# One block of level products per scan segment, from copies of each level's keys and queries

## The chip, the cores and the metric

The kernel runs on one core of a Trainium2 chip. The metric is the device time of one execution in microseconds (us). It is float32 in and out. One core has five engines that matter here, each with its own queue of instructions: PE multiplies matrices (PEld are its weight loads), DVE and ACT work on whole tiles of 128 partitions, POOL does a few copies, and SP issues the transfers (DMA).

## The reference: what is computed

One layer works on 2048 tokens of 1024 channels, with 256 context tokens ahead of them. After a modulated norm, one large projection gives the inputs of a gated linear recurrence (HGRN2, eight heads of 128 channels, both directions) and of a gated short convolution; a second projection brings both back, and a residual and a norm end it. The part that the change touches is the recurrence:

```python
bcum = jnp.cumsum(gc, axis=2)
diff = bcum[:, :, :, None, :] - bcum[:, :, None, :, :]
decay = jnp.where(mask, jnp.exp(jnp.where(mask, diff, 0.0)), 0.0)
attn = jnp.einsum('bhtk,bhsk,bhtsk->bhts', qc, kc, decay)
o = jnp.einsum('bhts,bhsv->bhtv', attn, vc) + jnp.einsum('bhtk,bhkv->bhtv', qc * jnp.exp(bcum), S)
```

For two tokens t and s of a chunk, attn is the product of query and key with a decay that depends on the channel and on all gates between s and t. The same is done backwards, and both directions are added.

## The kernel before, in words

**Stages.** The first 115 us load, norm and transpose the input. Then 32 windows follow, one for each head and each group of 512 tokens (a segment). In each window PE computes the projections of one segment, gates and values (and for some windows the output gates), while the scan of the segment before it is worked in between. After the heads come the convolution's windows (to about 1900 us) and the output projection.

**Projections.** Each f32 product is made of three f16 products (high x high, high x low, low x high), and each block of four is made of seven products by a Strassen-like scheme (`seven`, L830, its matmuls L839 to L841). One product is 4 x 3 = 12 matmuls of 128 x 256. Three PSUM banks of their own (sa, sb, sc) take them. ACT copies intermediate results out (`keep`, L844, its activation L846: tiles p and u) and DVE makes the outputs (L850). A product that adds to a bank can start only when the copy of what the bank held is made, and there is one other product between the two.

**The scan of a segment.** The products with decay are made in levels. At level lev, blocks of B = 2^lev tokens are paired. Keys and queries hold two copies, one for each direction (K and Q, 128 x 2 x 512). At each level, `level_k` (L409, its multiplication L414) and `level_q` (L416, L421) multiply by the decay of the half beside them in place, and `level_tot` (L423, L427) multiplies the decays of two halves together. What level lev needs is one product of the queries and keys as they are before that level's update, masked to the pairs of tokens that differ first at bit lev. For levels below 5 both directions fit in one product, when keys and queries are picked from the two copies in turn, B tokens from each: that is `mix`, an access pattern; for the keys ACT makes a copy in this order (km, `mixed`, L533, its activation L537), of which three rotate, and the queries are read by PE through the pattern.

- `diag` (L521): 16 matmuls of raw queries with the sum of the keys (128 x 32 by 128 x 32, f32; L528), an ACT copy into Ac (L530), and the copy km of level 0.
- `level` (L547), for lev 0 to 4: 16 matmuls (L554) into a bank of the pool `pa` (three banks, L77), the update, and DVE's masked copy into Ac (L557).
- `level5` (L560): 16 matmuls with 64 columns (L568), straight from K and Q, then the update.
- `level6` (L572): 8 matmuls with 64 x 64 (L578), the update, ACT's copy of the product into A (L582), and four POOL copies of Ac into A (L586).
- then keys are transposed (L593, L595), the states made (L602) and the output (L658, L659).

In the profile every f32 matmul is two instructions, so 16 of them are a group of 32. The tiles q and ks (raw queries, sum of keys), which `diag` reads, lie in a ring of ten buffers (`rp`, L68) that nearly all intermediate tiles share.

**What sets the order.** The steps of a segment stand in a list (`scan_steps`, L636), each with a weight from the table PACE (L45). `merge_steps` (L1278) turns the weights into places between 0 and 1, and `tick` (L1299), called after every three f16 matmuls, makes the steps whose place is passed. So the steps lie between the products of the window in the proportion of their weights. The framework below puts each engine's instructions into its queue and adds the waits; it may move an instruction ahead of others when its inputs are there.

Of the kernel before, what the change touches and what calls it, by code (L numbers as in the profile page):

```python
# [9 lines left out]
F32 = mybir.dt.float32  # L10
# [4 lines left out]
AF = mybir.ActivationFunctionType  # L15
# [4 lines left out]
P = 128  # L20
# [5 lines left out]
GW = 512  # L26
NG = SEQ // GW
NCH = GW // P
# [8 lines left out]
NSUB = 5  # L37
SB = 32
# [4 lines left out]


PACE = {"load": 0.0, "square": 0.22, "norm": 2.51, "turn": 9.58, "late": 4.0, "c_first": 1.5,  # L45
        "c_levels": 4.27, "c_keys": 0.85, "c_states": 0.31, "values": 0.65, "diag": 1.5, "level": 1.29,
        "level5": 2.6, "level6": 1.14, "keys": 1.0, "states": 2.0, "out": 0.53, "states2": 1.14,
        "out2": 1.0, "scale": 0.73, "turn_y": 0.54, "rstd": 0.63, "pause": 2.78}


def paced(weight, fn):

    return PACE.get(weight, weight), fn


def sub(t, off, dims):
    return bass.AP(t.tensor, t.offset + off, [list(t.ap[0])] + [list(d) for d in dims])
# [3 lines left out]
def hybrid_layer(ctx: ExitStack, tc, x, cx, w_ada, b_ada, w_in, w_out, fnorm_w, small_d, masks, ident_d, sel_d, out):  # L61
    nc = tc.nc
    V, S, G, PE, SY = nc.vector, nc.scalar, nc.gpsimd, nc.tensor, nc.sync
# [6 lines left out]
    scp = scg.__enter__()  # L70
# [20 lines left out]
    def pa_t(nm):  # L91
        return pa.tile([P, 512], F32, tag="pa", name=nm)
# [64 lines left out]
    par, at = {}, 0  # L157
# [50 lines left out]
    def norm_group(ntile, src, row0, m, nm, first_ops=None, space=q_tile):  # L208
# [61 lines left out]
        def turn(k):  # L270
# [8 lines left out]
            if first_ops is not None:  # L279
                for kk, h32 in ((k, a), (k + HK, b)):  # L280
                    SY.dma_start(Xd[:, kk], h32)
                    store(f"B{kk // HK + 1}1", k, h32[:, :HW], S)
                    store(f"B{kk // HK + 1}2", k, h32[:, HW:], G)
# [119 lines left out]
    mask = qp.tile([P, NSUB, SB], U8, name="mask", bufs=1)  # L403


    def mix(t, n, B, np_, off=0):
        return sub(t, off, [[2 * B, np_], [n + B, 2], [1, B]])

# [7 lines left out]
    def level_q(qf, cur, n, lev):  # L416
        B = 1 << lev
        np_ = n // (2 * B)
        nb = n // B
        m = mix(qf, n, B, np_)  # L420
        V.tensor_tensor(m, m, sub(cur, 1, [[2, np_], [nb - 1, 2], [0, B]]), ALU.mult)  # L421

    def level_tot(cur, tot, tot7, n, lev, off):  # L423
        nb = n >> lev
        dst = tot7 if lev == NLEV - 1 else tot[:, off:off + nb]
        dst = sub(dst, 0, [[1, nb]])
        V.tensor_tensor(dst, sub(cur, 0, [[2, nb]]), sub(cur, 1, [[2, nb]]), ALU.mult)  # L427
        return dst, off + nb
# [7 lines left out]
    class Seg:  # L436
# [81 lines left out]
                level_k(s.K, s.cur, s.n, lev)  # L518
                s.cur, s.off = level_tot(s.cur, s.tot, s.tot7, s.n, lev, s.off)

        def diag(s):  # L521
            s.start_levels()
            s.Ac = scp.tile([P, NCH, SB], F32, tag="Ac", name=f"Ac_{s.nm}")
            pt = pa_t(f"Ad_{s.nm}")
            for ch in range(NCH):
                for j in range(P // SB):
                    o = ch * P + j * SB
                    PE.matmul(pt[j * SB:(j + 1) * SB, ch * SB:(ch + 1) * SB], s.ks[:, o:o + SB], s.q[:, o:o + SB],  # L528
                              start=True, stop=True)
            S.activation(s.Ac, pt[:, :P].rearrange("p (c t) -> p c t", c=NCH), AF.Copy)  # L530
            s.mixed(0)

        def mixed(s, lev):  # L533
            B = 1 << lev
            n = s.n
            s.km = scp.tile([P, GW], F32, tag="km", name=f"km{lev}_{s.nm}", bufs=3)
            S.activation(sub(s.km, 0, [[2 * B, n // (2 * B)], [B, 2], [1, B]]), mix(s.K, n, B, n // (2 * B)), AF.Copy)  # L537

        def update(s, lev):
            n = s.n  # L540
            level_k(s.K, s.cur, n, lev)
            if lev + 1 < NSUB:
                s.mixed(lev + 1)
            level_q(s.qf, s.cur, n, lev)
            s.cur, s.off = level_tot(s.cur, s.tot, s.tot7, n, lev, s.off)

        def level(s, lev):  # L547
            n = s.n
            B = 1 << lev
            pt = pa_t(f"A{lev}_{s.nm}")  # L550
            for ch in range(NCH):
                for j in range(P // SB):
                    o = ch * P + j * SB
                    PE.matmul(pt[j * SB:(j + 1) * SB, ch * SB:(ch + 1) * SB], s.km[:, o:o + SB],  # L554
                              mix(s.qf, n, B, SB // (2 * B), o), start=True, stop=True)
            s.update(lev)
            V.copy_predicated(s.Ac, sub(mask, lev * SB, [[0, NCH], [1, SB]]),  # L557
                              pt[:, :P].rearrange("p (c t) -> p c t", c=NCH))

        def level5(s):  # L560
            n = s.n
            s.pt = pa_t(f"A5_{s.nm}")
            for ch in range(NCH):
                for j in range(P // SB):
                    i = j % 2
                    o = ch * P + j * SB
                    c0 = ch * P + (j - i) * SB
                    PE.matmul(s.pt[j * SB:(j + 1) * SB, c0:c0 + 2 * SB], s.K[:, i * n + o:i * n + o + SB],  # L568
                              s.qf[:, (1 - i) * n + c0:(1 - i) * n + c0 + 2 * SB], start=True, stop=True)
            s.update(5)  # L570

        def level6(s):  # L572
            n = s.n
# [62 lines left out]
    def scan_steps(h, s):  # L636
        prim = h.prim

        def states():
            pp = s.outer(prim)  # L640
            s.Ss = []
            Sp = h.S[prim]
            for ch in order(prim, NCH):
                s.Ss.append(Sp)
                Sn = new_state(f"S_{s.nm}_{ch}")
                V.scalar_tensor_tensor(Sn, Sp, s.decay(prim, ch), pp[:, ch * P:(ch + 1) * P], ALU.mult, ALU.add)
                Sp = Sn
            h.S[prim] = Sp
            psec = s.outer(1 - prim)
            s.Ts = scp.tile([P, GW], F32, tag="Tsec", name=f"Ts_{s.nm}", bufs=5)  # L650
            S.activation(s.Ts, psec, AF.Copy)

        def outp():
            po = px_t(f"o_{s.nm}")
            qo = (1 - prim) * GW
            for ch, Sp in zip(order(prim, NCH), s.Ss):
                sl = slice(ch * P, (ch + 1) * P)
                PE.matmul(po[:, sl], s.A[:, sl], s.v[:, sl], start=True, stop=False)  # L658
                PE.matmul(po[:, sl], s.qf[:, qo + ch * P: qo + (ch + 1) * P], Sp, start=False, stop=True)  # L659
            s.o = s.qf[:, qo:qo + GW]  # L660
            S.activation(s.o, po, AF.Copy)

        return ([paced("values", s.value_turn), paced("diag", s.diag)]
                + [paced("level", lambda lev=lev: s.level(lev)) for lev in range(NSUB)]
                + [paced("level5", s.level5), paced("level6", s.level6), paced("keys", s.key_turn), paced("states", states),
                   paced("out", outp)])

    ymax = cp.tile([P, 3 * HEADS, NG], F32, name="ymax")

# [428 lines left out]
    for hd in range(HEADS):  # L1098
# [4 lines left out]
        for i, g in enumerate(order(h.prim, NG)):  # L1103
            s = Seg(hd, g * GW, GW, 0, f"{hd}_{g}")
# [21 lines left out]
    for wi, (kind, a, i) in enumerate(stretch):  # L1126
# [31 lines left out]
        if wi > 0 and stretch[wi - 1][0] == "head":  # L1158
            _, pa_h, pi = stretch[wi - 1]
# [25 lines left out]
        if kind == "head" and a >= 6:  # L1185
            n = (a - 6) * NG + i
            extra += [paced(0.2, lambda k=k: wo_scan(k)) for k in (2 * n, 2 * n + 1)]
        if kind == "pair":
            n = (a - 1) * 2 + i
# [334 lines left out]
```

## Time and profile before

| | |
|---|---|
| runs, median of three | 2226.86 us (2222.09 to 2229.01) |
| profiled execution | 2224.16 us |
| its span | 2222.2 us |
| mean granted PE clock | 0.988 |
| PE busy | 2113.2 us |
| DVE busy | 1659.9 us |
| ACT busy | 1158.3 us |

The span is the time from the first to the last instruction. Busy time is the time in which an engine has an instruction; PE's includes the pipeline's tail, so a busy PE need not be at its peak. A row of a group gives line, engine, operation, output and inputs, shapes and count, then busy us, mean ns of one, idle time just before, and what ended it ("issue" means that nothing in the profile was waited for). A row in order of time gives start, length and the same names. A wait row reads: who <- for whom: us in total, times, longest us.

### The profile page before, as it was taken

To read this page: it belongs to the slowest core of one execution; us is meant where nothing else is said; L and a number is where in the kernel's file an instruction comes from. 1 tells how busy PE (TensorE), PEld (TensorE's weight loads), DVE (VectorE), ACT (ScalarE), POOL (GpSimd) and SP (SyncE) were. 2 spreads that over 40 slices of the span, in tenths; PEclk is the share of its full clock that TensorE was granted. 3 is DMA by queue.
4 is the path that set the end of the run, shared out by engine and by line. 5 is a ranking of instruction groups with operands and counts; after the bars stand their busy time and mean duration, and the time that the engine had idled before them with its cause. 6 is when DMAs were issued, how large, how long until landed. Compare 5 with 4: busy or idle time off the path is not lost.

```text
span 2222.2 us, 51962 instructions
## 1 busy us (share of the span) xinstructions
PE 2113.2 (95%) x21563; PEld 1466.6 (66%) x21563; DVE 1659.9 (75%) x3515; ACT 1158.3 (52%) x2313; POOL 112.5 (5%) x207
## 2 busy tenths in 40 slices
PE   4889899999999999999999999999999999999998
PEld 1767688888888888888888887444444444444443
DVE  6987877968779778788687786587678646677775
ACT  6655655665567555666676554354445313333332
POOL 0211100000000000000000000000000000000000
PEclk8889999999999999999999999999999999999999
DMA  8664343433243333333543357842343224633321
GB/s 324 223 212 169 103 137 103 153 95 117 82 158 112 106 120 119 108 111 122 191 134 131 126 183 248 240 137 101 108 138 116 68 90 157 232 106 122 120 99 57
DMA packets 191040, 309.89 MB, mean 139 GB/s; under 512 B 13138, under 2 KB 123090, under 8 KB 189012
## 3 DMA queue, kind: packets, MB, share of 16 engines
q1 hardware_dynamic: 188644, 302.64, 41.5%
q8 instruction: 169, 2.77, 0.5%
q10 hardware_dynamic: 2160, 3.93, 0.5%
q14 instruction: 67, 0.55, 0.1%
HBM read 241.50 MB, written 65.01 MB: 138 GB/s over the span
## 4 chain that ended last, share of the span: by engine, by line
PE 66%; DVE 15%; DMA 7%; ACT 6%; issue 4%; SPq 1%; POOL 1%; POOLq 0%; DVEq 0%; ACTq 0%
PE sa L839 8%; PE sa L841 7%; PE sa L840 7%; PE sb L839 4%; PE sb L840 3%; PE sb L841 3%; DMA ws_p<-in_w_in 3%; PE sa_o L839 2%; PE sa_o L841 2%; PE sa_o L840 2%; PE A L554 2%; PE T L602 2%; PE sc L839 2%; PE sc L841 2%; PE sc L840 2%
## 5 line engine op out<-in xcount | busy, mean ns | idle before, releaser
L840 PEld LDWEIGHTS <-e_p 128*128 128x128 f16 x1368 | 134.8, 99 | 66.8 <-issue 17.1
L414 DVE TENSOR_TENSOR K<-K,tot 128x512 f32<-128x512 f32 x192 | 132.0, 688 | 61.8 <-PE A L578 24.6
L839 PEld LDWEIGHTS <-e_p 128*128 128x128 f16 x1368 | 134.5, 98 | 60.2 <-issue 3.3
L841 PEld LDWEIGHTS <-e_p 128*128 128x128 f16 x1368 | 134.8, 99 | 53.1 <-issue 0.8
L421 DVE TENSOR_TENSOR Q<-Q,tot 128x512 f32<-128x512 f32 x192 | 132.6, 691 | 33.3 <-PE A L554 32.9
L537 ACT ACTIVATE km<-K 128x512 f32<-128x512 f32 x160 | 109.1, 686 | 86.3 <-DVE K L414 60.6
L840 PEld LDWEIGHTS <-whib_p 128*128 128x128 f16 x912 | 89.2, 98 | 45.5 <-issue 13.3
L586 POOL COPY A<-Ac 32x128 f32<-32x128 f32 x128 | 66.4, 519 | 1007.1 <-ACT A L582 649.2
L839 PEld LDWEIGHTS <-whib_p 128*128 128x128 f16 x912 | 89.1, 98 | 40.8 <-issue 3.7
L840 PEld LDWEIGHTS <-whia_p 128*128 128x128 f16 x912 | 89.3, 98 | 37.9 <-issue 6.3
L839 PEld LDWEIGHTS <-whia_p 128*128 128x128 f16 x912 | 89.2, 98 | 37.5 <-issue 0.8
L841 PEld LDWEIGHTS <-wloa_p 128*128 128x128 f16 x912 | 89.3, 98 | 34.3
L841 PEld LDWEIGHTS <-wlob_p 128*128 128x128 f16 x912 | 89.2, 98 | 34.3
L151 ACT ACTIVATE e_p<-ws_p,sc_p 128x512 f16<-128x512 f32 x108 | 77.2, 716 | 61.4 <-DVE ws_p L376 39.4
L341 ACT ACTIVATE junk<-ws_p 128x1024 f16<-128x1024 f32 x72 | 76.0, 1055 | 55.7 <-DMA ws_p<-in_w_in 55.2
L846 ACT ACTIVATE u<-sa,sx_w 128x256 f32<-128x256 f32 (+1 forms) x114 | 59.8, 524 | 70.9 <-PE sa L841 56.1
L554 PE MATMUL A<-Q,km 128*32 128x32 f32 x5120 | 77.9, 202 | 12.4 <-DVE Q L421 6.4
L554 PEld LDWEIGHTS A<-Q,km 128*32 128x32 f32 x5120 | 58.9, 112 | 46.4 <-issue 20.3
L762 ACT ACTIVATE cv<-c,small 128x512 f32<-128x512 f32 (+1 forms) x36 | 24.2, 671 | 109.2 <-DVE c L780 48.9
L152 DVE SCALAR_TENSOR_TENSOR e_p<-ws_p,sc_p,e_p 128x512 f16<-128x512 f32 x108 | 78.0, 743 | 2.5 <-ACT e_p L151 2.4
L846 ACT ACTIVATE p<-sb,sx_w 128x256 f32<-128x256 f32 (+1 forms) x114 | 59.3, 520 | 35.6 <-PE sb L841 34.0
L846 ACT ACTIVATE p<-sa,sx_w 128x256 f32<-128x256 f32 (+1 forms) x114 | 58.8, 516 | 32.2 <-PE sa L841 32.1
(865 smaller groups left out, 6881.7 us busy)
## 6 DMA issues: line engine op xcount, KB each, us to landing
ws_p<-in_w_in SPq DMA_DIRECT2D x72, 512.0 KB, 4.4
y_o<-yT SPq DMA_DIRECT2D x32, 512.0 KB, 3.8
wa<-in_w_ada SPq DMA_DIRECT2D x16, 512.0 KB, 5.4
Gd<-zs SPq DMA_DIRECT2D x32, 256.0 KB, 3.5
sg<-Gd SPq DMA_DIRECT2D x32, 256.0 KB, 4.1
yT<-y SPq DMA_DIRECT2D x32, 256.0 KB, 2.3
wos_a<-in_w_out SPq DMA_DIRECT2D x16, 512.0 KB, 4.6
yT<-sg SPq DMA_DIRECT2D x64, 128.0 KB, 2.6
```

Source lines behind the costliest of these rows:

```text
L151: S.activation(hi, src, AF.Copy, scale=st[:, 0:1])
L152: V.scalar_tensor_tensor(lo, src, st[:, 0:1], hi, ALU.mult, ALU.subtract)
L341: S.activation(junk.rearrange("p (k n) -> p k n", k=KT), stage[i], AF.Abs, accum_out=r)
L414: V.tensor_tensor(m, m, sub(cur, nb + 1, [[2, np_], [-(nb + 1), 2], [0, B]]), ALU.mult)
L421: V.tensor_tensor(m, m, sub(cur, 1, [[2, np_], [nb - 1, 2], [0, B]]), ALU.mult)
L537: S.activation(sub(s.km, 0, [[2 * B, n // (2 * B)], [B, 2], [1, B]]), mix(s.K, n, B, n // (2 * B)), AF.Copy)
L554: PE.matmul(pt[j * SB:(j + 1) * SB, ch * SB:(ch + 1) * SB], s.km[:, o:o + SB], mix(s.qf, n, B, SB // (2 * B), o), start=True, stop=True)
L586: G.tensor_copy(A3[js, :, js], s.Ac[js])
L839: PE.matmul(ps, hi[:, k], rh, start=start and k == 0, stop=False, skip_group_check=not start)
L840: PE.matmul(ps, hi[:, k], right(name, 1, k), start=False, stop=False, skip_group_check=not start)
L841: PE.matmul(ps, lo[:, k], rh, start=False, stop=k == nk - 1, skip_group_check=not start)
L846: S.activation(r, ps, AF.Copy, scale=sx)
```

## The change

`diag` becomes `begin_levels`, which multiplies nothing and makes the copies of level 0. `mixed` now serves keys and queries, and each level's copies have a buffer of their own (km0 to km4, qm0 to qm4). The steps of levels 0 to 4 are updates alone. A new step `blocks`, after them and after an empty step (`levels_end`), holds the products of the diagonal and of levels 0 to 4, each from its copies, into two banks, then level 5's products into a third, level 5's update, the copy of the diagonal and the five masked copies. PE reads the queries of levels 0 to 4 in a row of 32 from the copy, no longer through the pattern. ACT has 5 copies more per segment; the numbers of matmuls, updates and masked copies stay. A smaller DMA scratch is asked for; ten copies of 2 KB per partition stand where three stood.

```diff
-        def diag(s):
+        def begin_levels(s):
             s.start_levels()
-            s.Ac = scp.tile([P, NCH, SB], F32, tag="Ac", name=f"Ac_{s.nm}")
-            pt = pa_t(f"Ad_{s.nm}")
-            for ch in range(NCH):
-                for j in range(P // SB):
-                    o = ch * P + j * SB
-                    PE.matmul(pt[j * SB:(j + 1) * SB, ch * SB:(ch + 1) * SB], s.ks[:, o:o + SB], s.q[:, o:o + SB],
-                              start=True, stop=True)
-            S.activation(s.Ac, pt[:, :P].rearrange("p (c t) -> p c t", c=NCH), AF.Copy)
-            s.mixed(0)
-
-        def mixed(s, lev):
+            s.km, s.qm = [], []
+            s.mixed(s.km, "km", s.K, 0)
+            s.mixed(s.qm, "qm", s.qf, 0)
+
+        def mixed(s, to, nm, src, lev):
...
-            s.km = scp.tile([P, GW], F32, tag="km", name=f"km{lev}_{s.nm}", bufs=3)
-            S.activation(sub(s.km, 0, [[2 * B, n // (2 * B)], [B, 2], [1, B]]), mix(s.K, n, B, n // (2 * B)), AF.Copy)
+            t = scp.tile([P, GW], F32, tag=f"{nm}{lev}", name=f"{nm}{lev}_{s.nm}", bufs=1)
+            S.activation(sub(t, 0, [[2 * B, n // (2 * B)], [B, 2], [1, B]]), mix(src, n, B, n // (2 * B)), AF.Copy)
+            to.append(t)
 
         def update(s, lev):
             n = s.n
             level_k(s.K, s.cur, n, lev)
             if lev + 1 < NSUB:
-                s.mixed(lev + 1)
+                s.mixed(s.km, "km", s.K, lev + 1)
             level_q(s.qf, s.cur, n, lev)
+            if lev + 1 < NSUB:
+                s.mixed(s.qm, "qm", s.qf, lev + 1)
             s.cur, s.off = level_tot(s.cur, s.tot, s.tot7, n, lev, s.off)
 
-        def level(s, lev):
+        def blocks(s):
+
             n = s.n
-            B = 1 << lev
-            pt = pa_t(f"A{lev}_{s.nm}")
-            for ch in range(NCH):
-                for j in range(P // SB):
-                    o = ch * P + j * SB
-                    PE.matmul(pt[j * SB:(j + 1) * SB, ch * SB:(ch + 1) * SB], s.km[:, o:o + SB],
-                              mix(s.qf, n, B, SB // (2 * B), o), start=True, stop=True)
-            s.update(lev)
-            V.copy_predicated(s.Ac, sub(mask, lev * SB, [[0, NCH], [1, SB]]),
-                              pt[:, :P].rearrange("p (c t) -> p c t", c=NCH))
-
-        def level5(s):
-            n = s.n
+            pts = [pa_t(f"A{i}_{s.nm}") for i in ("d", "l")]
+            at = [pts[i // 4][:, i % 4 * P:(i % 4 + 1) * P] for i in range(NSUB + 1)]
+            for pt, k_, q_ in zip(at, [s.ks] + s.km, [s.q] + s.qm):
+                for ch in range(NCH):
+                    for j in range(P // SB):
+                        o = ch * P + j * SB
+                        PE.matmul(pt[j * SB:(j + 1) * SB, ch * SB:(ch + 1) * SB], k_[:, o:o + SB], q_[:, o:o + SB],
+                                  start=True, stop=True)
             s.pt = pa_t(f"A5_{s.nm}")
...
             s.update(5)
+            s.Ac = scp.tile([P, NCH, SB], F32, tag="Ac", name=f"Ac_{s.nm}")
+            S.activation(s.Ac, at[0].rearrange("p (c t) -> p c t", c=NCH), AF.Copy)
+            for lev in range(NSUB):
+                V.copy_predicated(s.Ac, sub(mask, lev * SB, [[0, NCH], [1, SB]]),
+                                  at[lev + 1].rearrange("p (c t) -> p c t", c=NCH))
...
-        return ([paced("values", s.value_turn), paced("diag", s.diag)]
-                + [paced("level", lambda lev=lev: s.level(lev)) for lev in range(NSUB)]
-                + [paced("level5", s.level5), paced("level6", s.level6), paced("keys", s.key_turn), paced("states", states),
-                   paced("out", outp)])
+        return ([paced("values", s.value_turn), paced("begin", s.begin_levels)]
+                + [paced("level", lambda lev=lev: s.update(lev)) for lev in range(NSUB)]
+                + [paced("levels_end", lambda: None), paced("blocks", s.blocks), paced("level6", s.level6),
+                   paced("keys", s.key_turn), paced("states", states), paced("out", outp)])
...
-    nc = bacc.Bacc("TRN2", target_bir_lowering=False, num_devices=1)
+    nc = bacc.Bacc("TRN2", target_bir_lowering=False, num_devices=1, dynamic_dma_scratch_size=1024)
```

In PACE, "diag" 1.5 and "level5" 2.6 give way to "begin" 1.0, "levels_end" 0.8 and "blocks" 2.4.

More of the change, by code (lines that the diff above doesn't have):

```diff
@@ L45 @@
 PACE = {"load": 0.0, "square": 0.22, "norm": 2.51, "turn": 9.58, "late": 4.0, "c_first": 1.5,
-        "c_levels": 4.27, "c_keys": 0.85, "c_states": 0.31, "values": 0.65, "diag": 1.5, "level": 1.29,
-        "level5": 2.6, "level6": 1.14, "keys": 1.0, "states": 2.0, "out": 0.53, "states2": 1.14,
+        "c_levels": 4.27, "c_keys": 0.85, "c_states": 0.31, "values": 0.65, "begin": 1.0, "level": 1.29,
+        "levels_end": 0.8, "blocks": 2.4, "level6": 1.14, "keys": 1.0, "states": 2.0, "out": 0.53, "states2": 1.14,
         "out2": 1.0, "scale": 0.73, "turn_y": 0.54, "rstd": 0.63, "pause": 2.78}
```

## The prediction

> **What bounds the kernel now.** I read the page's busy shares first, then the busy time by stretches, then the chain of work that ended last.
>
> ```profile
> PE 2113.2 (95%) x21563; PEld 1466.6 (66%) x21563; DVE 1659.9 (75%) x3515; ACT 1158.3 (52%) x2313; POOL 112.5 (5%) x207
> ...
> PE 66%; DVE 15%; DMA 7%; ACT 6%; issue 4%; SPq 1%; POOL 1%; POOLq 0%; DVEq 0%; ACTq 0%
> ```
>
> ```profile
> core 0: us, PE busy (x) PEld busy (x) DVE busy (x) ACT busy (x) POOL busy (x), PEclk, DMA share, GB/s
> ...
> 115.00:300.00 185.00, 162.21 (x2127) 135.41 (x2117) 150.16 (x349) 99.97 (x201) 29.09 (x52) 0.95 0.50 159
> 300.00:600.00 300.00, 295.78 (x4278) 254.53 (x4276) 235.93 (x536) 186.72 (x419) 16.36 (x32) 1.00 0.36 116
> ```
>
> ```profile
> L554 PEld LDWEIGHTS A<-Q,km x5120: 106/113/158, 114.6 to 1299.8; 128*32 128x32 f32 x197
> ```
>
> From 300 to 600 us PE is busy for 99% of the time at full granted clock, DVE for 79%, ACT for 62%, DMA for 0.36. This is the scan of the eight heads, whose level products run from 114.6 to 1299.8 us. So PE time taken away here shortens the run nearly one for one, as long as DVE and ACT keep up. Before 300 us PE idles 23 of 185 us; I expect less there.
>
> **What a level costs on PE.** The rows of PE in order of time, for four places: level 0, a later level, level 5, and a place where the diagonal and level 0 happen to stand together.
>
> ```profile
> 600.25 0.27 PE L841 MATMUL sa<-hop13T,wlob_p 128*128 128x256 f16 x1
> ...
> 600.58 0.27 PE L841 MATMUL sa<-hop13T,wlob_p 128*128 128x256 f16 x1
> 600.78 0.54 PE L554 MATMUL A<-Q,km 128*32 128x32 f32 x32
> 601.26 0.28 PE L839 MATMUL sb<-hop13T,whib_p 128*128 128x256 f16 x1
> ```
>
> ```profile
> 602.79 0.27 PE L841 MATMUL sa<-hop13T,e_p 128*128 128x256 f16 x1
> 603.00 0.47 PE L554 MATMUL A<-Q,km 128*32 128x32 f32 x32
> 603.39 0.28 PE L839 MATMUL sa<-hop13T,e_p 128*128 128x256 f16 x1
> ```
>
> ```profile
> 612.22 0.27 PE L841 MATMUL sa<-hop13T,wlob_p 128*128 128x256 f16 x1
> 612.43 0.65 PE L568 MATMUL A<-Q,K 128*32 128x64 f32 x32
> 613.01 0.28 PE L839 MATMUL sa<-hop13T,whib_p 128*128 128x256 f16 x1
> ```
>
> ```profile
> 1288.42 0.46 PE L528 MATMUL Ad<-q,ks 128*32 128x32 f32 x32
> 1288.69 0.56 PE L554 MATMUL A<-Q,km 128*32 128x32 f32 x32
> 1289.19 0.28 PE L839 MATMUL sa<-hop31T,e_p 128*128 128x256 f16 x1
> ```
>
> The f16 products start 0.11 us apart (600.25 to 600.58 is three steps). A later level puts 0.60 us between two f16 starts, so it costs 0.60 - 0.11 = 0.49. Level 0 costs 0.68 - 0.11 = 0.57, level 5 0.79 - 0.11 = 0.68. Where two narrow groups touch, the second starts 0.27 us after the first (1288.42 to 1288.69) and nothing idles between. So of 0.49 only 0.27 is the 32 instructions; the other **0.22 us is the seam**, paid on going from 128*128 to 128*32 operands and back.
>
> **The change, part by part.** Segments: the level row above counts 5120 instructions, 160 groups of 32, five for each of 32 segments.
>
> *Seams.* Before, a segment pays the diagonal 0.49, level 0 0.57, four levels 4 x 0.49 and level 5 0.68: 3.70 us, with seven seams. After, all seven follow one another: 6 x 0.27 + (0.68 - 0.22) + one seam of 0.22 = 2.30. Saved 1.40 us, of which 1.32 are six seams and 0.08 is level 0, whose queries are then read from a copy laid out in a row; I assume that takes away its excess over the other levels (bounds 0 and 0.08). 32 x 1.40 = 44.8 us; at 1288.42 one seam was gone already, and for a few such places I take off 1: **-44**. Bound from below: none of the level 0 part and a tenth of the seams lost, -38.
>
> *PE's waits at the levels.* What PE waited for before the level products (us, times), and their two group rows:
>
> ```profile
> L554 PEld LDWEIGHTS A<-Q,km 128*32 128x32 f32 x5120 | 58.9, 112 | 46.4 <-issue 20.3 <-DVE Q L421 7.2 <-ACT km L537 3.6
> L554 PE MATMUL A<-Q,km 128*32 128x32 f32 x5120 | 77.9, 202 | 12.4 <-DVE Q L421 6.4 <-ACT u L846 3.6 <-ACT km L537 1.3
> ```
>
> ```profile
>   issue: 20.3, 95
>   DVE Q L421: 13.7, 22
>   ACT u L846: 7.2, 2
>   ACT km L537: 4.9, 11
> ```
>
> A seam alone shows as 20.3/95 = 0.21 us of idle. In all 46.4 + 12.4 = 58.8 us; less 160 x 0.21 = 33.6, 25 us are true waits. The new block waits at most once per segment, for the queries and keys that level 4 has decayed; DVE reaches them earlier, since the masked copies come later and its queries no longer wait for PE (next part). Of the 25, the chain of levels has 13.7 - 22 x 0.21 + 4.9 - 11 x 0.21 = 11.7. I take half: **-6**; bounds 0 and -25.
>
> *Copies of the queries on ACT: 5 per segment, 160 in all.* The nearest row is the copy of the keys, same shape and stride:
>
> ```profile
> L537 ACT ACTIVATE km<-K 128x512 f32<-128x512 f32 x160 | 109.1, 686 | 86.3 <-DVE K L414 60.6 <-PE A L554 20.6 <-DVE tot L427 3.3
> ```
>
> 160 x 0.686 = 110 us more on ACT. The 32 segments lie in the 1185 us from 114.6 to 1299.8, 37 each, so 300 us hold about 8: 8 x 5 x 0.686 = 27 us, so ACT goes from 186 to 213, 71%. It is not the bound, but it stands in line before the copies that free PE's accumulators (u, p). The next product into the same bank comes one product later, 12 x 0.11 = 1.3 us; a copy later than that stops PE. Today:
>
> ```profile
> PE sa L839 <- ACT p L846: 5.3, 6, 2.9
> ...
> PE sb L839 <- ACT p L846: 3.6, 3, 3.1
> PE sa L839 <- ACT u L846: 3.6, 3, 2.9
> ```
>
> 12.5 us in the whole run. Bounds: 0, and one whole copy per segment held up, 32 x 0.686 = 22. I take half as much again as today, nearer to the row: **+7**.
>
> *DVE: which waits go and come.*
>
> ```profile
> DVE Q L421 <- PE A L554: 48.6, 51, 2.0
> ...
> DVE K L414 <- PE A L568: 24.0, 20, 2.1
> ...
> DVE K L414 <- ACT km L537: 12.6, 28, 1.1
> ```
>
> Today the update of the queries waits until PE has read them (48.6 us); then it waits for ACT's copy instead. Level 5's update of the keys waits for PE's level 5 products, and these now stand at the end of a block of 2.30 us instead of 0.68: up to 1.6 us more, 32 x 1.6 = 52 at most. Queued behind it on DVE are the other updates, the masked copies and the additions that empty PE's banks. What hides it is DVE's idle time, 64 us in 300, or 8 per segment; the 48.6 set free about pay for the 52. Charged **0**; with the cover gone, 52 over the run.
>
> *Moved only.* The row of the masked copies:
>
> ```profile
> L557 DVE COPY_PREDICATED Ac<-mask,A 128x128 f32<-128x128 uint8 x160 | 47.1, 294 | 0.0
> ```
>
> The diagonal's ACT copy and the five masked copies go behind the block and after level 5's update. Who waits for them is POOL's copy into A, and PE only at the output, about a third of a window later; 0, at most the 47 if DVE were full. The block takes three banks of the small PSUM pool, which is all of them, and holds the keys' sum and the raw queries in the ring half a window longer; only the first windows also transpose through that pool. 0; bounds, one block of 2.30 us won or lost in each of the first three windows, -7 and +7. The level products read SBUF tiles that exist once per level instead of three in rotation, so the keys' copies no longer wait for PE (20.6 us of ACT): slack, 0. No DMA is added or moved. [...]
>
> Sum: -44 - 6 + 7 = **-43 us**. The profiled execution took 2224.16 us for a span of 2222.2, so 2 us lie outside; 2224.16 - 43 = 2181. It stands 2.7 us under the median of the runs (2226.86), within their range, so I forecast **2182**.
>
> **Rivals.**
>
> *More is won.* All 25 us of waits go and ACT costs nothing: 44 + 25 = 69, 2155; about 2160 when the early part stays. Against it: 7.2 us of the waits are two places where ACT's u was late, which has nothing to do with levels.
>
> *ACT holds up PE.* Two copies' length per segment, 2 x 32 x 0.686 = 44 us: -44 - 6 + 44 = -6, 2218. For it: the copies of one level wait for DVE and block what stands behind them; the km row already has 60.6 us of ACT idling for DVE. Against: PE's whole loss to ACT is 12.5 us now. [...]
>
> *Slower: DVE and ACT in lockstep.* Each level's update on DVE now needs the ACT copy of the level before, for keys and for queries: ten hand-overs per segment. DVE is busy 235.9/8 = 29.5 us of a segment's 37.5; PE will need 37.5 - 1.4 = 36.1. So the case decides from (36.1 - 29.5)/10 = 0.66 us of DVE idle per hand-over, nearly a whole copy (0.686) uncovered. At 0.85 DVE needs 38.0 us, 0.5 more than now, 32 x 0.5 = 16: 2240. For it: only DVE's own next update covers a copy, and a foreign ACT instruction of 0.5 us in front uncovers it. Against: the keys' hand-over exists today and costs 12.6 us over 192 updates, 0.07 each, and even DVE's present 48.6 us for PE, over 160 updates, are 0.30 each.
>
> *Slower: the narrow products don't keep their pace.* If 0.27 per 32 only holds in short bursts, four column tiles at 112 ns a load give 28 ns an instruction: 192 x 28 = 5.4 us plus the 0.2 that level 5 takes beyond a level and the seam, 5.8 against 3.70, 32 x 2.1 = 67, 2291. Against: 64 in a row ran without slowing at 1288.42. [...]
>
> *It doesn't do what it says.* A row of DVE in order of time, and a piece of the chain (start, us, what):
>
> ```profile
> 653.68 1.14 DVE L414 TENSOR_TENSOR K<-K,f 128x512 f32<-128x512 f32 x1
> ```
>
> ```profile
> 658.87 0.39 PE Ad L528 x32
> ```
>
> The keys' level 0 update runs 5 us before the diagonal that the text puts ahead of it, so queue order is not the written order; if f16 products came between the groups, seams would stay: -6 + 7, 2225. Against: each group of before ran as 32 unbroken.
>
> **How the numbers follow.** Forecast 0.66 (its own range 2165 to 2200: -59 with 15 more of the waits won, -24 with no waits won and ACT at 22 or so), more won 0.07, ACT holds up PE 0.12, lockstep 0.08, pace 0.03, not done 0.04. What a measurement can tell from no change is 0.3%, 6.7 us. ACT's case spans 2200 to 2222, so half of it counts as faster: faster 0.66 + 0.07 + 0.06 = 0.79; same 0.06 + 0.04 = 0.10; slower 0.11. The range leaves out the slower cases, the undone one and the far end of the first: 2162 to 2213.
>
> **What would show it.** Right: one PE group of 192 level instructions per segment with one idle of 0.21 before it (7 us in all instead of 33.6 of seams); level instructions at 8 to 9 ns; the stretch from 115 to 1306 us about 40 shorter, the rest alike; two ACT groups of 160 copies near 0.69; DVE's wait for L554 gone. Wrong: PE waiting for ACT's u and p well over 20 us; DVE waiting for the copies over 100 us; PE idle before the block over 1 us per segment; the block over 3 us.

## The result and the profile after

The changed kernel takes 2285.59 us (median; 2274.43 to 2289.84), the kernel before 2226.86: a ratio of 1.0255, 95% interval 1.0233 to 1.0277. It is slower by 57 us. Its profiled execution took 2274.43 us for a span of 2272.6, the lowest of its runs, so the profile shows some 50 of the 57. One run of experiment 6 fell into a slower state and took 4233 us; it is left out there, and the time given is the median of the other three.

First the page of the changed kernel: busy times, and the chain by engine.

```profile
PE 2093.7 (92%) x21563; PEld 1473.8 (65%) x21563; DVE 1655.5 (73%) x3515; ACT 1247.5 (55%) x2473; POOL 117.7 (5%) x207
...
PE 52%; DVE 23%; ACT 11%; issue 6%; DMA 6%; SPq 2%; POOL 1%; POOLq 0%; DVEq 0%; ACTq 0%
```

PE is busy 19.5 us less than before (2113.2), although the run is 50 us longer. Its work did shrink; it stands still more often. The stretches of the head stage say where:

```profile
300.00:600.00 300.00, 278.85 (x4166) 246.66 (x4164) 229.35 (x521) 203.53 (x445) 19.46 (x32) 0.99 0.35 114
600.00:900.00 300.00, 280.16 (x4159) 248.09 (x4158) 219.80 (x489) 197.67 (x425) 17.87 (x32) 0.98 0.35 114
```

The second of them in the kernel before:

```profile
600.00:900.00 300.00, 296.71 (x4324) 255.66 (x4322) 234.87 (x523) 185.94 (x416) 16.66 (x32) 1.00 0.35 114
```

In 300 us PE now idles 21 us instead of 4, and its granted clock is 0.98 to 0.99 instead of 1.00. The trace's clock records show where: between 300 and 1350 us nine stretches of 3.4 to 6.8 us at half speed, in which the f16 products start 0.22 us apart, and none in the kernel before. DVE and ACT are not full (76 and 68% from 300 to 600). So neither of them became the bound by its busy time.

PE's weight loads for the narrow products, by group (the last column is idle time before them and what ended it). The first three are levels 0 to 4 in the first and second bank and the diagonal, all on one line now; L562 is level 5.

```profile
L554 PEld LDWEIGHTS Ad<-qm,km 128*32 128x32 f32 x3072 | 31.5, 108 | 2.0 <-issue 2.0
L554 PEld LDWEIGHTS Al<-qm,km 128*32 128x32 f32 x2048 | 23.1, 109 | 18.6 <-issue 16.9 <-ACT qm L532 1.6
L554 PEld LDWEIGHTS Ad<-q,ks 128*32 128x32 f32 x1024 | 11.9, 112 | 11.5 <-issue 7.2 <-ACT h_x L250 4.1 <-PE sc L840 0.2
L562 PEld LDWEIGHTS A<-Q,K 128*32 128x32 f32 x1024 | 18.8, 115 | 24.9 <-issue 24.5 <-DVE Q L421 0.4
```

The scan's last data are hardly waited for: 1.6 us for a copy of queries and 0.4 for the last queries in the whole run. But "issue", idle time that no semaphore explains, is 2.0 + 16.9 + 7.2 + 24.5 = 50.6 us. One seam of 0.21 per segment makes 32 x 0.21 = 6.7 of it. **Some 44 us are stops inside the block.** One block in order of time, on PE:

```profile
341.03 0.46 PE L554 MATMUL Ad<-q,ks 128*32 128x32 f32 x32
341.31 0.99 PE L554 MATMUL Ad<-qm,km 128*32 128x32 f32 x94
...
342.71 0.28 PE L562 MATMUL A<-Q,K 128*32 128x64 f32 x4
346.05 0.63 PE L562 MATMUL A<-Q,K 128*32 128x64 f32 x26 [3.06 <-issue]
346.62 0.28 PE L838 MATMUL sa<-hop6T,whib_p 128*128 128x256 f16 x1
```

The block starts at 341.03 and runs at the forecast pace: level 5 is reached 1.68 us later. Then, in level 5, of whose 32 products six are done, PE stands still for 3.06 us and goes on as if nothing had been missing. Apart from data on queue q1, what moved in this time is one packet; this is the DMA view of 343.8 to 343.9 us:

```profile
q8 instruction: 1, 0.02, 60.0%
```

From 331.6 to 343.8 us there is no packet of this queue. PE resumes some 2.2 us after the packet's start.

The other stops look alike. Idle times of more than 0.5 us, of PE's products and loads together, that nothing released: between 100 and 1360 us the trace has 17, 42 us in all, the longest 3.5 us, in or just behind 17 of the 32 blocks. Each ends 2.2 to 2.6 us after a q8 packet starts. The kernel before has two, 1.8 us, one of them behind a packet. Eight of the nine half-speed stretches begin during such a stop or at most 1.3 us after it. That the queue carries PE's instructions is shown by the first experiment below.

PE's waits for the ACT copies that free its banks (us, times, longest):

```profile
PE sa L838 <- ACT u L845: 12.2, 16, 1.6
PE sa L838 <- ACT p L845: 8.8, 11, 3.1
...
PE sb L838 <- ACT p L845: 7.1, 3, 2.8
```

28.1 us, 12.5 before. With all that PE waited for from ACT between 115 and 1360 us (idle times over 0.15 us), it is 48 us, 21 before.

### The profile page after: what moved, and what is told of

It is laid out like the page before. It is cut to its first block, busy times and chain, and to the rows that moved or that the text cites. A ratio compares the mean times of both kernels' runs of the same rounds, so it can differ in the third digit from the quotient of the medians.

```text
span 2272.6 us, 51989 instructions
## 1 busy us (share of the span) xinstructions
PE 2093.7 (92%) x21563; PEld 1473.8 (65%) x21563; DVE 1655.5 (73%) x3515; ACT 1247.5 (55%) x2473; POOL 117.7 (5%) x207
## 4 chain that ended last, share of the span: by engine, by line
PE 52%; DVE 23%; ACT 11%; issue 6%; DMA 6%; SPq 2%; POOL 1%; POOLq 0%; DVEq 0%; ACTq 0%
PE sa L838 7%; PE sa L840 6%; PE sa L839 6%; DVE K L414 4%; PE sb L838 3%; PE sb L839 3%; PE sb L840 3%; DVE Q L421 2%; PE sa_o L838 2%; PE sa_o L840 2%; PE sa_o L839 2%; DMA ws_p<-in_w_in 2%; ACT km L532 2%; DVE e_p L152 2%; ACT qm L532 2%
## 5 line engine op out<-in xcount | busy, mean ns | idle before, releaser
L532 ACT ACTIVATE qm<-Q 128x512 f32<-128x512 f32 x160 | 110.2, 689 | 51.5 <-DVE Q L421 39.1
L585 POOL COPY A<-Ac 32x128 f32<-32x128 f32 x128 | 71.5, 558 | 1052.0 <-ACT A L581 816.0
L151 ACT ACTIVATE hiS_o<-y_o,sc_y 128x1024 f16<-128x1024 f32 x32 | 36.8, 1149 | 66.8 <-PE sc_o L839 23.4
```

Of the source, the lines that this page charges most:

```text
L151: S.activation(hi, src, AF.Copy, scale=st[:, 0:1])
L532: S.activation(sub(t, 0, [[2 * B, n // (2 * B)], [B, 2], [1, B]]), mix(src, n, B, n // (2 * B)), AF.Copy)
L585: G.tensor_copy(A3[js, :, js], s.Ac[js])
```

## The experiments

All times are set against runs of the kernel before on the same chip in the same session, whose medians were 2226.75 to 2229.32 us. The theories: **A**, the run of narrow products outruns the supply of instructions to PE; **B**, PE waits in the block for the last queries and keys; **C**, the copies on ACT are the loss.

**1. A run without new data: the diagonal six times over.** The kernel before, with

```diff
-            for ch in range(NCH):
+            for ch in [c_ for _ in range(6) for c_ in range(NCH)]:
                 for j in range(P // SB):
                     o = ch * P + j * SB
                     PE.matmul(pt[...], s.ks[:, o:o + SB], s.q[:, o:o + SB], start=True, stop=True)
```

> The kernel before, with the diagonal's 16 matmuls issued six times over in one piece (the repeats write the same numbers again). Added work: 5 x 0.27 us x 32 segments = 43 us, no copy, wait or bank added. Theory A, a long run of narrow products outruns the supply of instructions to PE: the trace of the change has 26 stops of 1 to 3 us put down to issue, 47 us in all, in or just behind the block, so this one stops in the same way: 2227 + 43 + about 45 = 2315 (2295 to 2335), with issue stops of 1 to 3 us in the run of L528 or just behind it. Theory B, the stops in the block are waits for the last queries and keys: no such data is waited for here, 2227 + 43 = 2270 (2262 to 2278).

Measured: 2332.36 us, ratio 1.0465 (1.0436 to 1.0495), 103 us more and in theory A's range. (Counted as above, once for products and loads together, the stops of the change are 17 and 42 us, not 26 and 47; here 22 follow a packet, 45 us.) One of its runs on PE, its group row and the DMA view of 510.6 to 510.7 us:

```profile
507.46 2.35 PE L528 MATMUL Ad<-q,ks 128*32 128x32 f32 x163
512.92 0.65 PE L528 MATMUL Ad<-q,ks 128*32 128x32 f32 x29 [3.11 <-issue]
```

```profile
L528 PEld LDWEIGHTS Ad<-q,ks 128*32 128x32 f32 x6144 | 61.5, 110 | 40.6 <-issue 36.7 <-ACT q L504 2.0 <-ACT h_x L250 0.9
```

```profile
q8 instruction: 1, 0.02, 60.1%
```

All 192 products of this run have the same inputs, and 163 of them ran. The stop of 3.1 us in front of the other 29 can't be a wait for data: B falls. PE resumes at 512.92, again some 2.3 us after a packet's start. The page's row of the queue (packets, MB, share), in the kernel before and in this one:

```profile
q8 instruction: 169, 2.77, 0.5%
```

```profile
q8 instruction: 209, 3.42, 0.6%
```

This kernel has 5120 products and 5120 weight loads more than the kernel before: 40 packets for 10240 instructions, 256 each. The kernel before agrees: 2 x 21563 = 43126 products and loads, 168.5 packets of 256, for 169 packets. So the queue brings PE's instructions, about 256 a packet. At the f16 pace, two instructions in 0.11 us, a packet lasts 14 us; at the narrow pace, two in 8.5 ns, it lasts 1.1 us, less than the 2.2 us from a packet's start to the next instruction. The block has 2 x 224 = 448 instructions.

**2. The same work in short runs.** The kernel before, with each of the five level products twice over, so that runs are of 64:

```diff
-            for ch in range(NCH):
+            for ch in [c_ for _ in range(2) for c_ in range(NCH)]:
                 for j in range(P // SB):
                     o = ch * P + j * SB
                     PE.matmul(pt[...], s.km[:, o:o + SB], mix(s.qf, n, B, SB // (2 * B), o), start=True, stop=True)
```

> The kernel before, with each of the five level products of a segment issued twice over, so 64 narrow instructions stand together instead of 32: the same added work of 43 us as six diagonals in one piece, in five small pieces. Theory A (supply of instructions): 64 in a row ran without a stop before, so nearly no issue stops: 2227 + 43 = 2270 (2262 to 2282). Theory B: the same, 2270. Together with the run in one piece it tells the length of the run from the amount of work.

Measured: 2290.06 us, 1.0263 (1.0239 to 1.0287), 61 us more, past the range of both theories.

```profile
L554 PEld LDWEIGHTS A<-Q,km 128*32 128x32 f32 x10240 | 111.0, 112 | 61.7 <-issue 30.9 <-DVE Q L421 15.3 <-ACT u L846 3.3
```

Issue is 30.9 us instead of 20.3, the wait for queries 15.3 instead of 7.2. Seven stops of 0.5 to 1.4 us, 7 us in all, end 2.3 to 2.7 us after a packet starts: where groups of 64 come close together they are nearly, not wholly, supplied. Still, the same 5120 products cost 42 us less than in one run.

**3. Runs of 96.** The diagonal three times over, otherwise as in 1.

> The kernel before with the diagonal's products issued three times over in one piece (96 narrow instructions; the repeats write the same numbers). Added work 2 x 0.27 x 32 = 17 us; the spread repeats cost 61 for 43 of work, so 24 by their rate: 2253 if 96 in a row are supplied as well as 64. Theory A, with stops growing with the length of the run (12 us of issue at runs of 64, 48 at 192 and 224): some 20 us of stops, 2229 + 17 + 20 = 2266 (2250 to 2280), with stops in fewer segments than for 192.

Measured: 2253.17 us, 1.0123 (1.0110 to 1.0136), the time for runs that are supplied as well as those of 64, but also within theory A's range. The trace decides:

```profile
L528 PEld LDWEIGHTS Ad<-q,ks 128*32 128x32 f32 x3072 | 30.3, 109 | 8.8 <-issue 5.4 <-ACT q L504 2.0 <-ACT h_x L250 0.9
```

Issue of 5.4 us is no more than one seam per segment, and none of the run's stops over 0.5 us lies in these products. The stops do not begin at 96; they are there at 192.

**4. The copies alone.** The kernel before, with copies of keys and queries in buffers of their own and each level's products read from them at the old places:

```diff
-                    PE.matmul(pt[...], s.km[:, o:o + SB],
-                              mix(s.qf, n, B, SB // (2 * B), o), start=True, stop=True)
+                    PE.matmul(pt[...], s.km[lev][:, o:o + SB],
+                              s.qm[lev][:, o:o + SB], start=True, stop=True)
```

> The kernel before with the copies of the queries alone: each level's keys and queries are copied by ACT into buffers of their own, and each level's products are made from the copies at their old places, not in one block. 160 ACT copies more, no long run of narrow products. Theory A (supply of instructions is most of the loss, ACT's lateness the rest: PE's idle for ACT's u, p and the like rose from some 24 to 54 us): 2227 + 25 = 2252 (2240 to 2265). Theory C, ACT's added copies are the whole loss: at least 2285, as the seams are not saved here. If the copies cost nothing: 2222 to 2230.

Measured: 2245.21 us, 1.0065 (1.0046 to 1.0084), 14 us more, in theory A's range. C as the whole loss falls; the copies are a smaller part.

**5. The block alone.**

```diff
         def begin_levels(s):
             s.mixed(s.km, "km", s.K, 0)
-            s.mixed(s.qm, "qm", s.qf, 0)
...
-            for pt, k_, q_ in zip(at, [s.ks] + s.km, [s.q] + s.qm):
+            for pt, k_, q_ in zip(at, [s.ks] + s.km, [s.q] + [s.qf] * NSUB):
```

> The changed kernel without the copies of the queries: the block's level products read the queries as they are after level 4's update, so what is computed for pairs within 32 tokens isn't the reference's; PE's instructions are as many and in one block as in the change. Theory A (supply of instructions): the stops of 47 us and the clock's half-speed stretches stay, ACT's lateness goes: 2285 - 30 = 2255, at the least still above the kernel before (2228 to 2265). Theory C (ACT's copies are the whole loss): the block alone wins what was forecast for the seams, 2227 - 44 = 2183 (2175 to 2200).

Measured: 2274.47 us, 1.0194 (1.0163 to 1.0225), 43 us more; theory A had allowed up to 2265. Block 1.9% and copies 0.65% together make about the 2.55% of the change. Its level groups:

```profile
L551 PEld LDWEIGHTS Al<-Q,km 128*32 128x32 f32 x2048 | 22.8, 109 | 18.1 <-issue 18.0
...
L559 PEld LDWEIGHTS A<-Q,K 128*32 128x32 f32 x1024 | 19.1, 116 | 25.1 <-issue 24.7 <-DVE K L414 0.4
```

The stops are those of the change (16.9 and 24.5 there).

**6. The block in two parts.** The diagonal, levels 0 and 1 after level 1's update; levels 2 to 4 and level 5 at the block's place:

```diff
-                + [paced("level", lambda lev=lev: s.update(lev)) for lev in range(NSUB)]
+                + [paced("level", lambda lev=lev: s.update(lev)) for lev in range(2)]
+                + [paced(0.0, lambda: s.part(0))]
+                + [paced("level", lambda lev=lev: s.update(lev)) for lev in range(2, NSUB)]
```

> The changed kernel with its block in two parts: diagonal, level 0 and level 1 (96 narrow instructions) right after level 1's update, levels 2 to 4 and level 5 (128) at the block's place, with f16 products and three updates between. Same copies, same work, one seam more. Theory A (a long run of narrow products outruns the instruction supply): the supply catches up between the parts, issue stops shrink from 47 to about 15 us, and the clock keeps its full speed: 2229 + 16 (copies, as measured alone) - 35 (five seams) + 20 = 2230 (2212 to 2250). If the length of the run doesn't matter, the time of the change: 2285 (2270 to 2292).

Measured: 2249.00 us, 1.0096 (1.0076 to 1.0116): some 36 us less than the change, and still 22 above the kernel before, at the upper end of the range.

```profile
L552 PEld LDWEIGHTS A<-qm,km 128*32 128x32 f32 x5120 | 52.9, 109 | 17.2 <-issue 11.4 <-ACT qm L532 5.7
L564 PEld LDWEIGHTS A<-Q,K 128*32 128x32 f32 x1024 | 16.9, 109 | 0.8 <-issue 0.4 <-DVE tot L427 0.3
L552 PEld LDWEIGHTS A<-q,ks 128*32 128x32 f32 x1024 | 12.0, 112 | 11.5 <-issue 7.7 <-ACT h_x L250 3.8
```

Issue is 19.5 us, of which two seams per segment make 13.4. Of the stops over 0.5 us two are left, 2.4 us, and with them went most of the loss: runs of 96 and 128 are supplied. What remained was not explained by the copies' 14 us against five seams saved, which led to the next runs. In the trace it is ACT: PE idles 59 us for it, 48 in the change and 21 before.

**7. Masked copies later in the text.** In the change DVE idles in front of the masked copies, since they wait for the block. The step of level 6 was to take them, the same lines in another place:

```diff
-            s.Ac = scp.tile([P, NCH, SB], F32, tag="Ac", name=f"Ac_{s.nm}")
-            S.activation(s.Ac, at[0]..., AF.Copy)
-            for lev in range(NSUB):
-                V.copy_predicated(...)
...
         def level6(s):
             s.update(6)
...
```

> The changed kernel with the diagonal's ACT copy and the five masked copies moved from the block's step to the step of level 6, so that they stand less far ahead in DVE's and ACT's queues. In the change DVE waited 21 us (10 times, up to 3.8 us) in front of the masked copies for ACT's copy of the diagonal, which waits for the block. If this wait holds up PE's accumulators and makes the part of the loss that neither the stops for instructions nor the copies explain: 2286 - 12 = 2274 (2262 to 2279). If DVE had the time: 2286 (2279 to 2292).

Measured: 2284.64 us, 1.0257 (1.0232 to 1.0281), no difference. But the edit did not do what it says. DVE's row in the change and in this kernel:

```profile
L568 DVE COPY_PREDICATED Ac<-mask,Ad 128x128 f32<-128x128 uint8 x96 | 28.5, 297 | 27.6 <-ACT Ac L566 26.1
```

```profile
L580 DVE COPY_PREDICATED Ac<-mask,Ad 128x128 f32<-128x128 uint8 x96 | 28.7, 298 | 28.0 <-ACT Ac L578 26.1
```

The idle time is the same: the order in the queue is not that of the text, and the copies were put ahead again. The run says nothing on its question.

**8. Masked copies held back by a dependency,** in the two-part form; they stand in level 6's step, as in 7:

```diff
+            zero = sp.tile([P, 1], F32, tag="zero", name=f"zero_{s.nm}", bufs=2)
+            V.tensor_scalar(zero, s.K[:, 0:1], 0.0, None, ALU.mult)
-            S.activation(s.Ac, at[0]..., AF.Copy)
+            S.activation(s.Ac, at[0]..., AF.Identity, bias=zero)
```

> The block in two parts, with the diagonal's copy and the five masked copies held back until level 6's update of the keys is made: the diagonal's copy adds a zero that is computed from those keys (one small DVE instruction per segment). In the two parts DVE idles 74 us in front of the masked copies, behind which other work stands; before the change it was 0. If that wait is the part of the loss that is neither stops for instructions nor added copies: 2251 - 20 = 2231 or less (2215 to 2236), DVE's idle there gone. If ACT's copies are the whole rest: 2251 (2245 to 2257).

Measured: 2238.81 us, 1.0052 (1.0037 to 1.0067), 10 us less than 6 and just past the range. The row of the masked copies in 6 and here:

```profile
L570 DVE COPY_PREDICATED Ac<-mask,A 128x128 f32<-128x128 uint8 x160 | 47.5, 297 | 74.2 <-ACT Ac L568 47.3 <-PE A L552 25.4
```

```profile
L585 DVE COPY_PREDICATED Ac<-mask,A 128x128 f32<-128x128 uint8 x160 | 47.3, 296 | 2.9 <-ACT Ac L582 2.4
```

71 us of DVE's idle time went, and 10 us of the run, nearly half of the rest. But PE hardly waited less: its idle times over 0.15 us between 115 and 1360 us fell from 76 to 73 us. What fell is the time that half-speed stretches cost there (half of PE's time in them), from 18 to 6 us, and the granted clock was 0.981 to 0.983 in the runs of 6 and 0.983 to 0.988 here. So the gain is mostly clock; why holding back the copies raised it is not shown.

**9. Two parts without the query copies.**

```diff
             s.mixed(s.km, "km", s.K, 0)
-            s.mixed(s.qm, "qm", s.qf, 0)
...
-            if lev + 1 < NSUB:
-                s.mixed(s.qm, "qm", s.qf, lev + 1)
...
-            for pt, k_, q_ in list(zip(s.at, ..., ([s.q] + s.qm)[...]))[3 * i:]:
+            for pt, k_, q_ in list(zip(s.at, ..., ([s.q] + [s.qf] * NSUB)[...]))[3 * i:]:
```

> The block in two parts without the copies of the queries: levels 0 to 4 read the queries as they are at that time, so pairs within 32 tokens are not the reference's; PE's work is as before. If ACT's copies are the whole rest: five seams won, 2227 - 35 + 5 = 2197 to 2205. If the masked copies' wait is the rest and copies cost the 16 us that they cost alone: 2251 - 16 = 2235 (2228 to 2242).

Measured: 2225.88 us, 0.9995 (0.9983 to 1.0007): 23 us less than 6, more than the 14 that the copies cost alone. It lies between the two forecasts. Why the copies cost more here no run shows; and without them PE still idles 43 us for ACT, twice as much as in the kernel before.

**10. The copies on POOL.** The query copies alone, in the two-part form and in the change itself:

```diff
-            S.activation(to_, mix(src, n, B, n // (2 * B)), AF.Copy)
+            G.tensor_copy(to_, mix(src, n, B, n // (2 * B)))
```

> The block in two parts, with the five copies of the queries made by POOL (5% busy) instead of ACT. If the 24 us by which the two parts on ACT stayed above the kernel before are ACT's lateness (PE waited 52 us for ACT's u, p, vT_c and h_x there, 24 before), this gives the five seams: 2227 - 35 + 10 = 2202 (2192 to 2218). POOL's nearest row is 0.55 to 0.79 us for half the elements, so a copy takes 1.1 to 1.6 us, and level updates wait for it; if that lateness replaces ACT's: 2227 to 2250.

> The changed kernel, its block in one piece, with the copies of the queries on POOL. The results are the reference's, unlike the block without copies. Theory A: the stops for instructions stay and ACT's lateness goes, so the time of the block without copies: 2272 (2258 to 2282). If the copies on ACT were most of the loss: below 2250.

Measured: 2277.77 us, 1.0242 (1.0222 to 1.0262), and 2326.41 us, 1.0446 (1.0431 to 1.0460). Both are far worse than with ACT and outside all that was expected. A copy on POOL is not slow:

```profile
L534 POOL COPY qm<-Q 128x512 f32<-128x512 f32 x160 | 132.8, 830 | 610.8 <-DVE Q L496 269.4 <-DVE Q L421 150.1 <-PE o L663 44.7
```

830 ns against ACT's 689. The kernels are some 30 and 41 us over the forms with ACT, and it is not the stops: the block in one piece has 17 that follow a packet, 41 us, as in the change. DVE is late. In the two-part form PE's idle times rose from 76 to 101 us, although those for ACT fell from 59 to 44; DVE ended 13 with ACT's copies and 33 with POOL's, of them, and in front of the transposes of the context's keys new ones appeared (first ACT's form, then POOL's):

```profile
L594 PEld LDWEIGHTS kT_c<-ident,K_c 128*128 128x128 f32 x32 | 3.7, 141 | 0.8 <-PE sc L844 0.8
```

```profile
L598 PEld LDWEIGHTS kT_c<-ident,K_c 128*128 128x128 f32 x32 | 3.4, 141 | 15.2 <-issue 15.2
```

These seven carry no releaser, but each ends 0.12 us after DVE's last update of those keys. DVE's updates of the keys (192) took 721 ns on average in this run and 689 with ACT: 75 that ran at the same time as a POOL copy took 776 ns, the others 686. That is 6 us; what else makes DVE late stays open.

**11. Small groupings.** Since 64 in a row hardly stop and a pair needs a copy for one of its two levels alone, three kernels were built from the kernel before: the diagonal beside level 0 alone (no copy added), and three pairs (diagonal and 0, 1 and 2, 3 and 4; copies of the queries of levels 1 and 3), the pairs also with their copies on POOL.

```diff
+            if lev in (1, 3):
+                s.update(lev)
+                return
...
+            if lev == 0:
+                s.products(pair[0], s.ks, lambda o: s.q[:, o:o + SB])
+            else:
+                s.products(pair[0], s.kms[lev - 1], lambda o: s.qms[lev - 1][:, o:o + SB])
+            s.products(pair[1], s.km, lambda o: mix(s.qf, n, B, SB // (2 * B), o))
```

> The kernel before with the diagonal's products moved beside level 0's, and nothing else: raw queries, sum of keys and level 0's copy of the keys exist then anyway, so no copy is added. One seam per segment fewer: 0.22 x 32 = 7 us, less the few places where they stood together already: 2223 (2217 to 2229). If seams are not what PE loses at a narrow group: 2229.

> Runs of two: the diagonal's products stand with level 0's, level 1's with level 2's, level 3's with level 4's, so no run is longer than 64, and only levels 1 and 3 need a copy of their queries (64 ACT copies more, not 160). Three seams per segment fewer. Theory A: 3 x 0.22 x 32 = 21 us won, 0.4 x 16 = 6 lost to the copies, about 5 to the supply of instructions: 2229 - 10 = 2219 (2208 to 2229). If any added copy or any grouping costs more than its seam: 2229 or more.

> Runs of two with the two copies of the queries made by POOL instead of ACT. With ACT as before and three seams fewer: 2227 - 21 + 4 = 2210 (2202 to 2218). If ACT's 64 copies cost nothing in the runs of two: 2219 as with ACT; if POOL's slower copies hold up the updates: 2219 to 2235.

Measured: the first pair 2222.36 us, 0.9980 (0.9971 to 0.9989); three pairs 2219.61, 0.9969 (0.9957 to 0.9981), with POOL 2218.27, 0.9964 (0.9951 to 0.9976), the last just past its range. They are below both kernels, 0.2 to 0.4% below the kernel before. One seam per segment is worth 4.5 us net, less than the 7 reckoned but in the range. Three would be 13 at that rate, less the copies; 7 and 8 were measured.

## Why the prediction was wrong, point by point

- **What bounds the kernel: right.** PE did, and time in which PE stands still is lost: of the 103 us that experiment 1 took more, 45 are stops and 43 the added products (an estimate, 5 x 0.27 x 32).
- **Seams: the mechanism right, the size too large, and the sum built on it wrong.** The narrow products ran on without a seam and at the pace read from 1288.42: level 5 was reached 1.68 us after the block's start, six groups of 0.28. But the step "all seven follow one another ... 2.30 us" failed. The pace came from 64 in a row and was carried over to 224. PE's instructions came in packets of about 256, and the runs of 192 and 224 used them faster than they came: 42 to 44 us of stops in the block or just behind it, where 44 were to be won. The one place in the trace with 64 in a row could not show the limit.
- **Waits at the levels (-6): too large at the source.** I added the idle time of PE and of its weight loads, 12.4 and 46.4, but these are largely the same gaps: the changed kernel lists the stops of level 5 under both, as 22.5 us for PE and 24.5 for its loads. With 46.4 alone, true waits were 46.4 - 33.6 = 13 us, not 25. That the -6 itself came out near what was won is luck, half of a doubled sum: the loads waited 7.2 + 3.6 = 10.8 us for queries and keys before, seams included, and 2.0 after.
- **ACT's copies (+7): too small.** 14 alone and 23 in the two-part form, about the upper bound of 22. PE's idle time for ACT was 48 us in the change, 28 in the block without the copies and 21 before. So the rival "ACT holds up PE", with 0.12, named a part of the loss that is there.
- **Masked copies moved at no cost: doubtful.** I named who waits for them, and not that they themselves wait, in DVE's queue, for the whole block, with other work behind them (27.6 us of DVE's idle time in the change). Holding them back was worth 10 us in the two-part form, mostly as clock; for the block in one piece no run shows it.
- **DVE's wait at level 5 (0) and the lockstep rival: not borne out.** DVE waited 15.9 us for the query copies and 33.5 for the key copies, where the case needed 0.66 us at each of 320 hand-overs.

```profile
DVE K L414 <- ACT km L532: 33.5, 39, 2.7
...
DVE Q L421 <- ACT qm L532: 15.9, 36, 1.1
```

- **The rival "the narrow products don't keep their pace"** had 0.03. It named the right place, bursts, and the time it gave, 2291, is near the 2286, but for another reason: each product keeps its pace, and the run is interrupted. Its 28 ns an instruction was my estimate, and no run shows it: the 192 products of six groups started in 1.68 us, 8.75 ns each. It was put aside with the 64 in a row of 1288.42, a run too short to show the stops. What bears on them is the 40 packets for 10240 instructions of experiment 1: the block's 448 instructions in some 2 us are more than one packet of 256, and at the 17 stops of the change PE went on 2.2 to 2.6 us after a packet's start.

The parts as an estimate, from the two profiles between 115 and 1360 us: PE's idle times over 0.15 us grew from 36 to 107 us, those without a releaser from 2 to 43, those for ACT from 21 to 48, those for DVE from 12 to 14. Half-speed stretches cost 9 us before and 20 after. Together 82 us were lost, and the profiled run is 50 longer, so some 30 were won. Six seams at the 4.5 us of the first pair are 27; the forecast was 44. So the stops are about half of what was lost, and the seams seem to be worth less than the rows of single places said; why is not shown.

## What to carry to other kernels

Putting small products together saved the seam between operand shapes here, 4.5 us for one seam per segment, but a run of very short instructions has to be fed: count its instructions (loads too), and set the packets it needs against the time in which they come. Here runs of up to 128 products lost at most 7 us in the whole kernel, and runs of 192 and more 41 to 47 us, in stops of up to 4 us. When an instruction is moved behind a long step on another engine, ask what stands behind it in its own queue; and look at the queue in the trace, since an edit of the text may not have moved it (27.6 and 28.0 us of idle time in experiment 7).

## What the runs showed of the hardware that was not expected

- PE stopped when its instructions ran out: 17 times, 42 us, in the change. A packet carried about 256 of them (40 packets for 10240), and PE resumed 2.2 to 2.6 us after the packet's start at all 17.
- The stops showed as "issue", idle time without a releaser, and those of level 5 were counted under both PE (22.5 us) and its loads (24.5 us).
- They seem to cost clock too: the granted clock fell from 1.00 to 0.98 between 600 and 900 us, and eight of nine half-speed stretches began during a stop or at most 1.3 us after it. That one causes the other is argued from the times alone.
- POOL copied 128x512 f32 in 830 ns, but the kernels with POOL's copies were some 30 and 41 us slower than with ACT's 689 ns. DVE was late there; its updates beside a POOL copy took 776 ns instead of 686, which explains a part.
